# Different 64-byte starts for the weight-part buffers of a one-core hybrid decoder layer

## The chip, the core and the metric

The kernel runs on one core of one Trainium2 chip. The metric is the device time of one execution in microseconds; times of before are the median of three runs. The core has TensorE (matrix products), VectorE, ScalarE, GpSimd and SyncE, each with its own stream of instructions, and 16 DMA engines that they share. On-chip memory has 128 partitions; an address in this text is an offset in bytes within a partition, the same in all of them.

## The reference

One layer of a decoder trunk for 16 meta tokens and 256 tokens with 2048 channels, all in float32:

```python
u = rms_norm(h, g_pre_mix[l])
proj = u @ w_in[l]
z_pool, v_conv, g_conv, gate_a, gate_b = jnp.split(proj, splits, axis=-1)
y_a = causal_multiscale_pool(z_pool, w_pool_grp[l], pool_scale[l]) @ w_pool_out[l]
y_b = conformer_conv(v_conv, g_conv, w_dw[l], b_dw[l],
                     conv_ln_g[l], conv_ln_b[l]) @ w_conv_out[l]
m = jax.nn.sigmoid(gate_a) * y_a + jax.nn.sigmoid(gate_b) * y_b
h = h + rms_norm(m @ w_o[l], g_post_mix[l])
u = rms_norm(h, g_pre_mlp[l])
f = jnp.square(jax.nn.relu(u @ w_up[l])) @ w_down[l]
h = h + rms_norm(f, g_post_mlp[l])
```

w_in has 2048 x 7168 elements, w_up 2048 x 8192 and w_down 8192 x 2048. The result drops the meta tokens.

## The kernel before, in words

All weights are streamed once, in chunks of 1 MB (128 partitions x 2048 numbers, `CK` x `CW` or an equal area). A list `stream` holds them in order: w_in for the convolution's value and gate and for the pool (acc_v, acc_g, acc_z), w_in for the two gates (acc_gate), w_pool_grp, w_pool_out (acc_po), w_conv_out (acc_co), w_o (acc_o, acc_o_last), and then four rounds of w_up (acc_up) and w_down (acc_dn, at the end acc_f_last).

For accuracy each float32 operand is split in two parts of the faster type fp32r, a high part and the rest. `open_chunk` (line 136) takes the next chunk: SyncE loads it into a `raw` buffer (line 153), ScalarE writes the high part `hi` (line 156), VectorE writes `lo = raw - hi` (line 159). The activations (u, y, s_act, m, f_act) have two parts as well, at index a = 0 and 1. Three products are computed: high by high, high by low, low by high.

A matmul has a stationary operand (128 x 128 numbers, loaded by a weight load of its own) and a moving operand (128 x N, streamed through). Which part of a chunk is which depends on the stage:

- `block_t` (line 566; acc_gate, acc_po, acc_co, acc_o, acc_dn, acc_f_last): the activation is stationary, the weight chunk moves, mostly with N = 512. For each k the order is (a = 0, hi), (a = 0, lo), (a = 1, hi).
- `mm3` (line 308; acc_v, acc_g, acc_z): the weight chunk is stationary, u moves with N = 272. The order is (hi, a = 0), (hi, a = 1), (lo, a = 0).
- `mm2` (lines 313 and 318; acc_up): the weight chunk is stationary, u2 (the memory of m) moves; hi with both parts at once (N = 512), then lo with a = 0 (N = 256).

The order on each engine is that of the program, written out by hand; `fetch` (line 176) opens and splits chunks two ahead of the one that it hands out. VectorE's and ScalarE's other work stands between in queues (`pending`, `late`). Raws, hi and lo have three buffers each. Around the change from w_o to w_up, two chunks (numbers 90 and 91) get their parts in one buffer each of the tags s0 and s1 of the pool `big`, not in `parts`. Chunk 89 is the first of w_up and is in `parts`; 92 is the first after these two. Tags s0 and s1 later hold f_act, the MLP's activation: f_act0 (s0) has the first half of k of a round, f_act1 (s1) the second. Further lines named below: 652 and 641 (normalisation on VectorE), 796 and 800 (u2).

Pools follow one another in memory, in the order const, big, raws, parts, tmp; within a pool tags follow in the order of their first use. In the program before, u and m begin at 71,488, f_act1 (s1) at 106,304, f_act0 (s0) at 122,688, the raws at 139,072, and the parts at 163,648 and every 8,192 after it (three hi, then three lo). The tag of y and s_act begins at 21,376 and 37,760. A row of u for one k and a has 272 numbers, 1,088 = 17 x 64 bytes; acc_gate reads u from its 17th number on, 64 bytes into the row. The rows of m, y, s_act and f_act have 256 numbers for each k and a.

Of the kernel before, what the change touches and what calls it, by code (L numbers as in the profile page):

```python
# [9 lines left out]
F32R = mybir.dt.float32r  # L10
# [4 lines left out]
P = 128  # L15
CK = 4
CW = 512
# [5 lines left out]
def hybrid_block(ctx: ExitStack, tc: tile.TileContext, ins: dict, out: bass.AP):  # L23
# [3 lines left out]
    T, D = x.shape  # L27
# [3 lines left out]
    KD = D // P  # L31
    w_in = ins["w_in"][0]
    w_grp = ins["w_pool_grp"][0]
    NG, GD, _ = w_grp.shape
# [14 lines left out]
    const = ctx.enter_context(tc.tile_pool(name="const", bufs=1))  # L49
    big = ctx.enter_context(tc.tile_pool(name="big", bufs=1))  # L50
    raws = ctx.enter_context(tc.tile_pool(name="raws", bufs=3))
    parts = ctx.enter_context(tc.tile_pool(name="parts", bufs=3))
    tmp = ctx.enter_context(tc.tile_pool(name="tmp", bufs=2))
    psA = ctx.enter_context(tc.tile_pool(name="psA", bufs=6, space=PSUM))
    psB = ctx.enter_context(tc.tile_pool(name="psB", bufs=2, space=PSUM))
# [1 line left out]
    def f32(ap):  # L57
        return ap.bitcast(F32)
# [74 lines left out]
    opened = []  # L133
    at = {"n": 0}

    def open_chunk():
        n = at["n"]
        at["n"] += 1
        src, (rows, width) = stream[n]
        raw = raws.tile([P, CK * CW], F32, tag="raw", name=f"raw_{n}")  # L140
        if n in spare:
            both = big.tile([P, 2, CK * CW], F32R, tag=spare[n], name=f"parts_{n}")
            hi, lo = both[:, 0, :], both[:, 1, :]
        else:
            hi, lo = (parts.tile([P, CK * CW], F32R, tag=tag, name=f"{tag}_{n}")
                      for tag in ("hi", "lo"))
        raw, hi, lo = (t.rearrange("p (k c) -> p k c", k=rows) for t in (raw, hi, lo))
        pieces = rows if n < FIRST + 1 else 1
        k = rows // pieces
        loads = 4 if n < FIRST else 1  # L150
        for i in range(loads):
            sl = slice(i * rows // loads, (i + 1) * rows // loads)
            nc.sync.dma_start(raw[:, sl, :], src[:, sl, :])

        def high(sl):
            nc.scalar.copy(hi[:, sl, :], raw[:, sl, :])  # L156

        def low(sl):
            nc.vector.tensor_sub(lo[:, sl, :], raw[:, sl, :], f32(hi[:, sl, :]))  # L159

        def piece(i):
            def f():
                sl = slice(i * k, (i + 1) * k)
                high(sl)
                low(sl)
            return f
        todo = [piece(i) for i in range(pieces)]
        if n in spare:
            todo = [lambda: high(slice(0, rows)), lambda: low(slice(0, rows))]
        opened.append((hi, lo, todo))  # L170
# [5 lines left out]
    def fetch(ahead=2):  # L176

        for c in range(ahead + 1):
            if c == len(opened) and at["n"] < len(stream):
                open_chunk()  # L180
            if c < len(opened):
                split_pieces(c)
        flush()
        return opened.pop(0)[:2]
# [47 lines left out]
    for b in range(XB):  # L232
        load_x(b)
        if b % 2 == 0:
            open_chunk()
# [164 lines left out]
    def pieces_to(n):  # L400

        while first["split"] < min(n, (FIRST + 1) * HALF[0]):
            c = first["split"] // HALF[0]
            if c == at["n"]:
                open_chunk()
            opened[c][2].pop(0)()
            first["split"] += 1
# [212 lines left out]
    hi, lo = fetch()  # L620
# [185 lines left out]
    f_act = []  # L806
# [92 lines left out]
    for k0 in (3 * CK, 3 * CK + 2):  # L899
# [4 lines left out]
    up_high(2, 1)  # L904
    up_low(2)
    hi, lo = fetch()
    f_act += [big.tile([P, KD // 2, 2, T], F32R, tag=f"s{b}", name=f"f_act{b}")
              for b in range(2)]
    for j, acc in enumerate(accs):
        for k in range(CK):  # L910
            kk = 3 * CK + k
# [68 lines left out]
    n = KD // CK - 3  # L980
    for kc in range(n):
        hi, lo = fetch()
# [12 lines left out]
    for h, cs in enumerate(col_halves):  # L995
# [3 lines left out]
        s = tmp.tile([P, HALF_CW], F32, tag="sum", name=f"last_{h}")  # L999
# [37 lines left out]
```

## Time and profile before

| | us |
|---|---|
| median of three runs | 1256.38 |
| lowest, highest | 1256.12, 1256.86 |
| the profiled execution | 1256.48 |
| its span, first to last instruction | 1254.7 |

| engine | busy us | share of the span |
|---|---|---|
| TensorE matmuls (PE) | 1241.1 | 99% |
| TensorE weight loads (PEld) | 1064.9 | 85% |
| VectorE (DVE) | 810.2 | 65% |
| ScalarE (ACT) | 542.4 | 43% |

The DMA engines moved 237 MB at a mean of 189 GB/s. The granted TensorE clock is full throughout.

Matmuls are pipelined, so the duration that the profile gives one of them (around 390 ns for 512 columns) is not what it adds to the time. What it adds is the distance from one start to the next. That is read from the chain of work that ended last, whose rows give a start, a length and a count, or from rows of the timeline.

### The profile page before, as it was taken

How to read it: one execution, taken by the hardware profiler on the slowest of the kernel's cores; microseconds unless marked ns; L12 is line 12 of the kernel's file. 1: busy time of each engine (PE TensorE's matmuls, PEld its weight loads, DVE VectorE, ACT ScalarE, POOL GpSimd, SP SyncE). 2: the span in 40 equal slices, each digit the busy share in tenths (PEclk: the TensorE clock that was granted, in tenths of full speed). 3: DMA queues.
4: the chain of work that ended last, by engine and by line, in shares of the span. 5: the costliest groups of instructions: out<-in, count | busy, mean ns of one | idle time of the engine just before them, and what ended most of it. 6: DMA issues, size and time to landing. Idle time of an engine off the chain costs nothing.

```text
span 1254.7 us, 15708 instructions
## 1 busy us (share of the span) xinstructions
PE 1241.1 (99%) x6562; PEld 1064.9 (85%) x6562; DVE 810.2 (65%) x938; ACT 542.4 (43%) x571; POOL 6.1 (0%) x18
## 2 busy tenths in 40 slices
PE   8999999999999999999999999999999999999997
PEld 7999988888888888898888888888888888888886
DVE  5799978999676664585654456554465544556555
ACT  6633334443583434555533344433344433435432
POOL 1000000000000000000000000000000000000000
PEclk9999999999999999999999999999999999999999
DMA  7655555555547655646555655556656556556551
GB/s 244 207 184 180 168 176 194 194 178 200 171 165 285 214 205 201 201 140 197 189 181 200 201 175 194 183 188 200 198 171 202 180 190 200 181 189 198 179 192 68
DMA packets 130759, 237.24 MB, mean 189 GB/s; under 512 B 3985, under 2 KB 29905, under 8 KB 130160
## 3 DMA queue, kind: packets, MB, share of 16 engines
q1 hardware_dynamic: 129280, 230.70, 56.2%
q0 software_dynamic: 768, 4.35, 0.9%
q10 hardware_dynamic: 640, 1.19, 0.3%
q8 instruction: 51, 0.84, 0.3%
q14 instruction: 20, 0.16, 0.0%
HBM read 234.12 MB, written 2.10 MB: 188 GB/s over the span
## 4 chain that ended last, share of the span: by engine, by line
PE 98%; DVE 0%; DMA 0%; ACT 0%; DVEq 0%; ACTq 0%; issue 0%
PE acc_dn L566 26%; PE acc_up L313 19%; PE acc_gate L566 14%; PE acc_up L318 10%; PE acc_o L566 5%; PE acc_v L308 4%; PE acc_z L308 4%; PE acc_g L308 4%; PE acc_co L566 4%; PE acc_po L566 4%; PE acc_f_last L566 2%; PE acc_o_last L566 2%; PE xt L256 1%; DMA m_in<-in_meta_dram 0%; PE ht L790 0%; PE mt L685 0%
## 5 line engine op out<-in xcount | busy, mean ns | idle before, releaser
L159 DVE TENSOR_TENSOR lo<-raw,hi 128x2048 fp32r<-128x2048 f32 (+1 forms) x236 | 495.1, 2101 | 364.0 <-ACT hi L156 363.0
L156 ACT CAST hi<-raw 128x2048 fp32r<-128x2048 f32 (+1 forms) x236 | 413.9, 1757 | 574.0 <-PE acc_dn L566 191.1
L313 PE MATMUL acc_up<-m,hi 128*128 128x512 f32 (+1 forms) x1008 | 344.8, 395 | 0.0
L566 PE MATMUL acc_dn<-hi,f_act 128*128 128x512 f32 x960 | 296.4, 389 | 0.0
L318 PE MATMUL acc_up<-m,lo 128*128 128x256 f32 x992 | 265.8, 281 | 0.0
L313 PEld LDWEIGHTS acc_up<-m,hi 128*128 128x128 f32 x1008 | 183.2, 188 | 39.5
L566 PEld LDWEIGHTS acc_dn<-hi,f_act 128*128 128x128 f32 x960 | 180.2, 188 | 37.4
L318 PEld LDWEIGHTS acc_up<-m,lo 128*128 128x128 f32 x992 | 186.2, 189 | 6.3
L566 PE MATMUL acc_dn<-lo,f_act 128*128 128x512 f32 x480 | 186.7, 389 | 0.0
L566 PE MATMUL acc_gate<-hi,u 128*128 128x512 f32 x512 | 161.8, 396 | 0.0
L376 DVE SCALAR_TENSOR_TENSOR c<-a,taps,c 128x256 f32<-128x256 f32 x240 | 115.4, 483 | 6.6
L566 PEld LDWEIGHTS acc_gate<-hi,u 128*128 128x128 f32 x512 | 96.0, 188 | 22.4
L566 PEld LDWEIGHTS acc_dn<-lo,f_act 128*128 128x128 f32 x480 | 90.1, 188 | 18.6
L566 PE MATMUL acc_gate<-lo,u 128*128 128x512 f32 x256 | 99.9, 390 | 0.0
L566 PE MATMUL acc_o<-hi,m 128*128 128x512 f32 x192 | 59.5, 390 | 0.0
L566 PEld LDWEIGHTS acc_gate<-lo,u 128*128 128x128 f32 x256 | 48.1, 188 | 11.7
L308 PE MATMUL acc_v<-u,hi 128*128 128x272 f32 x256 | 51.1, 297 | 0.0
L308 PE MATMUL acc_g<-u,hi 128*128 128x272 f32 x256 | 48.3, 288 | 0.0
L308 PE MATMUL acc_z<-u,hi 128*128 128x272 f32 x256 | 48.3, 288 | 0.0
L566 PEld LDWEIGHTS acc_o<-hi,m 128*128 128x128 f32 x192 | 36.0, 188 | 7.4
L566 PE MATMUL acc_co<-hi,s_act 128*128 128x512 f32 x128 | 41.1, 397 | 0.0
L308 PEld LDWEIGHTS acc_v<-u,hi 128*128 128x128 f32 x256 | 40.9, 193 | 0.0
(222 smaller groups left out, 1062.8 us busy)
## 6 DMA issues: line engine op xcount, KB each, us to landing
raw<-in_w_up_dram SPq DMA_DIRECT2D x64, 1024.0 KB, 5.4
raw<-in_w_down_dram SPq DMA_DIRECT2D x64, 1024.0 KB, 5.1
raw<-in_w_in_dram SPq DMA_DIRECT2D x54, 1024.0 KB, 5.1
raw<-in_w_o_dram SPq DMA_DIRECT2D x16, 1024.0 KB, 5.1
raw<-in_w_pool_out_dram SPq DMA_DIRECT2D x8, 1024.0 KB, 5.2
raw<-in_w_conv_out_dram SPq DMA_DIRECT2D x8, 1024.0 KB, 5.2
x_in<-in_x_dram SPq DMA_DIRECT2D x4, 512.0 KB, 8.5
raw<-in_w_in_dram SPq DMA_DIRECT2D x8, 256.0 KB, 7.5
```

The source lines that it names most:

```text
L156: nc.scalar.copy(hi[:, sl, :], raw[:, sl, :])
L159: nc.vector.tensor_sub(lo[:, sl, :], raw[:, sl, :], f32(hi[:, sl, :]))
L256: nc.tensor.transpose(pt[:, M + t * P:M + (t + 1) * P], x_in[:, t, sl], ident)
L308: nc.tensor.matmul(acc, w[:, k[0], cs], act[:, k[1], a, off:], start=first and n == 0, stop=last and n == 2)
L313: nc.tensor.matmul(acc.rearrange("p (a t) -> p a t", a=2)[:, :, ts], hi[:, k[0], cs], act[:, k[1], :, off + ts.start:off + ts.stop], start ...
L318: nc.tensor.matmul(acc[:, :T], lo[:, k[0], cs], act[:, k[1], 0, off:], start=False, stop=False)
L376: nc.vector.scalar_tensor_tensor(c, conv["a"][:, q, i:i + T], taps[:, q, i:i + 1], c, op0=ALU.mult, op1=ALU.add)
L566: nc.tensor.matmul(acc, act(kk)[:, a_, ts_], w_[:, k, :], start=kk == 0 and n == 0, stop=kk == nk - 1 and n == 2)
```

## The change

The six buffers of `parts` get a tag each (hi0 to hi2, lo0 to lo2), with a room that is 0, 64, 128 or 192 bytes larger than the part, and the part lies at the end of its room. Which one a chunk gets is its number modulo 3. Before, each tag's three buffers were taken in turn by the chunks that use them, and chunks 90 and 91, which use none, weren't counted. f_act0 gets a room 64 bytes larger, too, and lies at its end, so the tag s0 grows by 64 bytes; f_act1 stays as it was. Everything behind a larger room in memory moves by as much.

```diff
-    parts = ctx.enter_context(tc.tile_pool(name="parts", bufs=3))
+    parts = ctx.enter_context(tc.tile_pool(name="parts", bufs=1))
...
+    SHIFT = {"hi0": 0, "hi1": 64, "hi2": 128, "lo0": 64, "lo1": 192, "lo2": 0}
+
+    def part_tile(tag, n):
+        key = f"{tag}{n % 3}"
+        room = parts.tile([P, CK * CW + SHIFT[key] // 4], F32R, tag=key, name=f"{tag}_{n}")
+        return room[:, SHIFT[key] // 4:]
+
     def open_chunk():
...
-            hi, lo = (parts.tile([P, CK * CW], F32R, tag=tag, name=f"{tag}_{n}")
-                      for tag in ("hi", "lo"))
+            hi, lo = (part_tile(tag, n) for tag in ("hi", "lo"))
...
-    f_act += [big.tile([P, KD // 2, 2, T], F32R, tag=f"s{b}", name=f"f_act{b}")
-              for b in range(2)]
+    for b in range(2):
+        room = big.tile([P, KD * T + 16 * (1 - b)], F32R, tag=f"s{b}", name=f"f_act{b}")
+        f_act.append(room[:, 16 * (1 - b):].rearrange("p (k a t) -> p k a t", k=KD // 2, a=2))
```

## The prediction

> **What bounds the kernel now.** I read the page first (share of each engine, then the chain that ended last), then the chain in order of time, then windows, waits and timelines of single stages.
>
> ```profile
> span 1254.7 us, 15708 instructions
> PE 1241.1 (99%) x6562; PEld 1064.9 (85%) x6562; DVE 810.2 (65%) x938; ACT 542.4 (43%) x571; POOL 6.1 (0%) x18
> PE 98%; DVE 0%; DMA 0%; ACT 0%; DVEq 0%; ACTq 0%; issue 0%
> ```
>
> The reader is to see that TensorE is never short of work: 98% of the chain is matmuls. So the time can move only if a matmul itself takes another time, or if a new wait opens in front of one. The profiled execution took 1256.48 us, 1.8 us more than its span and 0.1 us above the median of the three runs (1256.38); I make the sum against 1256.48.
>
> The chain in order of time gives the pace of each stage: length divided by count.
>
> ```profile
> 80.56 12.05 PE acc_g L308 x96
> 164.94 150.47 PE acc_gate L566 x648
> 350.67 44.80 PE acc_po L566 x192
> 425.22 11.20 PE acc_co L566 x48
> 449.22 59.86 PE acc_o L566 x264
> 625.38 87.05 PE acc_dn L566 x384
> 802.87 87.05 PE acc_dn L566 x384
> ```
>
> All but the first row are 512-column matmuls of one form, and their paces differ: acc_dn 226.7 ns, acc_o 226.7, acc_po and acc_co 233.3, acc_gate 232.2. The 272-column acc_g runs at 125.5. The two acc_dn pieces also give the up stage between them: 802.87 - (625.38 + 87.05) = 90.44 us for 256 pairs of a 512- and a 256-column matmul, 353.3 ns a pair.
>
> What makes 226.7 into 233.3? Not the clock and not the neighbours' work:
>
> ```profile
> 350.00:400.00 50.00, 50.00 (x219) 40.18 (x218) 34.12 (x28) 29.95 (x31) 1.27 (x2) 1.00 0.59 199
> 450.00:500.00 50.00, 50.00 (x222) 41.42 (x221) 23.95 (x15) 21.30 (x18) 0.30 (x1) 1.00 0.61 212
> 650.00:700.00 50.00, 50.00 (x222) 41.41 (x221) 24.26 (x14) 17.22 (x9) 0.00 (x0) 1.00 0.58 192
> ```
>
> The columns are the window, its length, then busy time and count of TensorE, weight load, VectorE, ScalarE and GpSimd, granted clock, DMA share, GB/s. The clock is 1.00 in all three, and DMA is 0.58 to 0.61. VectorE is busier in the first, which lies in acc_po, but acc_co at 425 us has the same 233.3 as acc_po at 350, whatever VectorE does beside them. What does separate the stages is where their operands begin. I count places in 64-byte units modulo 8. Before, every weight part (hi, lo), m and f_act begin at place 5, and y and s_act at place 6. While one matmul streams its moving rows, the weights of the next are being loaded (weight load is busy 85% of the span beside a busy TensorE). Let d be the place of those weights minus the place of the moving rows. acc_dn and acc_o have d = 0 throughout; acc_po and acc_co have d = 1. In the gates u has rows of 17 x 64 bytes, so d walks through all places: odd for two of the three matmuls of a k, even for the third.
>
> **Prices.** For 512 columns: d = 0 costs 226.7 ns; d odd 233.3 (6.67 more). Even but not zero follows from the gates: 3 x 232.2 - 2 x 233.3 = 230.0, 3.3 more. For this last the ends are 0 (it is like zero) and 6.67 (like odd); I take the 3.3 of the gates.
>
> On two reading streams the Trainium skill has a rule, in "TensorE: Matmul & The Clock Gate", Part 2, step 1: the array reads moving rows and weights through two independent ports, so loading the next weights takes nothing from the running matmul. By it d is worth nothing and the sum would be 0. The trace disagrees: 226.7 against 233.3 for one form. The same page's "Back-to-back issue gap" gives N/2.4 + 2.5 ns, 215.8 ns for 512 columns; no stage here comes under 226.7.
>
> **The change part by part.** No instruction, load or queue entry is added or removed. What moves are addresses, and one choice of buffer.
>
> *Where things come to lie.* With 64 bytes more in tag s0 the raws begin at place 6 and the parts pool at place 6; adding the room sizes in order of first use (hi0, lo0, hi1, lo1, hi2, lo2) gives hi0 6, lo0 7, hi1 0, lo1 3, hi2 5, lo2 5. f_act0 goes to 6, f_act1 stays at 5, u and m at 5, y and s_act at 6. The order of use is my assumption from the other tags of this kernel. Each stage meets all three buffers in turn, so I average over them.
>
> *acc_dn and acc_f_last (1440 + 144 matmuls).* Moving hi, lo, hi against f_act at 6 (first half of k) or 5. d for (hi, lo, hi): buffer 0: 0, 7, 0 and 7, 6, 7; buffer 1: 6, 3, 6 and 5, 2, 5; buffer 2: 1, 1, 1 and 0, 0, 0. Of 18: nine odd, four even, five zero. (9 x 6.67 + 4 x 3.3) / 18 = 4.07 ns each; x 1584 = +6.4 us. Ends: even free +5.3, even like odd +7.6.
>
> *acc_o (384).* m at 5: 7, 6, 7; 5, 2, 5; 0, 0, 0. Four odd, two even: 3.7 ns, +1.4 us (1.1 to 1.7).
>
> *acc_po, acc_co (384).* Weights at 6, all odd before; after: 0, 7, 0; 6, 3, 6; 1, 1, 1. Four of nine get cheaper, two by 6.67 and two by 3.3: -0.9 us (-1.1 to -0.6).
>
> *acc_gate (768).* With buffers 0 and 1 all three d are even: 230.0 in place of 232.2 for 512 matmuls, -1.1 us (-2.8 if even is free, at 226.7).
>
> *acc_v, acc_g, acc_z (1056 past the start).* Here u moves and hi, lo are loaded. One of three d was odd; with buffers 0 and 1 all three are: 1056 x 2/3 x 2/3 = 469 more odd ones. No row prices an odd d at 272 columns by itself: lower end 0, since the stage's 125.5 is one mean over odd and even; upper end 6.67 from acc_po, 3.1 us. The stage's own row is nearer in form but silent, so I take the middle, +1.6.
>
> *acc_up (976 pairs).* All d are 0 before, yet a pair takes 353.3. Zero-distance matmuls elsewhere say 226.7 + 120.0 = 346.7, the 120.0 from the last block:
>
> ```profile
> 1239.75 0.28 PE L566 MATMUL acc_f_last<-lo,f_act 128*128 128x256 f32 x1
> ...
> 1241.19 0.28 PE L566 MATMUL acc_f_last<-lo,f_act 128*128 128x256 f32 x1
> ```
>
> (five such rows 0.36 us apart, three matmuls each). So an up pair already pays 6.67 that I can't explain. With buffers 0 and 1 (651 pairs) the wide matmul gets d even (2 or 6) and the narrow one d odd (1 or 3). Upper end 3.3 + 6.67 = 10 ns a pair, +6.5 us; lower end, the unexplained 6.67 goes, -4.3 us. I take half the upper, +3.3: the narrow matmul is nearest to the 272-column stage, where I also took half.
>
> *The buffer choice.* Two chunks (90 and 91) lie in s0 and s1 and use no slot. Before, the slots simply went on; after, the chunk's number decides, so chunk 92 gets the buffer of chunk 89 and not that of 87. Its cast must wait for the last read of hi 89, its subtraction for the last of lo 89.
>
> ```profile
> 540.82 2.08 PE L318 MATMUL acc_up<-m,lo 128*128 128x256 f32 x16
> ```
>
> ```profile
> 544.39 1.93 ACT L156 CAST hi<-raw 128x2048 fp32r<-128x2048 f32 x1
> ```
>
> ```profile
> 547.29 2.28 DVE L159 TENSOR_TENSOR lo<-raw,hi 128x2048 fp32r<-128x2048 f32 x1
> ```
>
> The reads of hi 89 are over as the lo group starts (about 541.1), those of lo 89 at 542.9; the writers come at 544.39 and 547.29 anyway, 3.3 and 4.4 us later. Cost 0. Were that cover gone, chunk 92 would come later by what exceeds it, and with it what stands behind the cast and the subtraction on ScalarE and VectorE, the next u2 tiles and chunk 93.
>
> *VectorE, ScalarE and DMA.* Their operands come to lie apart, too.
>
> ```profile
> L159 DVE TENSOR_TENSOR lo<-raw,hi 128x2048 fp32r<-128x2048 f32 x212 | 485.6, 2291 | 363.6 <-ACT hi L156 362.7
> L159 DVE TENSOR_TENSOR lo<-raw,hi 128x256 fp32r<-128x256 f32 x24 | 9.4, 417 | 0.3 <-ACT hi L156 0.3
> L652 DVE TENSOR_TENSOR c<-c,sq 128x1024 f32<-128x1024 f32 x2 | 2.5, 1226 | 4.3 <-ACT c L647 4.3
> ```
>
> L159, with all operands at one place, takes (2291 - 417) / 1792 = 1.046 ns a column, so 1220 for 1024; L652, whose sq lies one place beyond c, takes 1226. A slower subtraction or cast would cost nothing, since the cast idles until TensorE frees its buffer:
>
> ```profile
> ACT hi L156 <- PE acc_dn L566: 191.1, 57, 3.5
> ACT hi L156 <- PE acc_up L313: 146.1, 45, 3.8
> ACT hi L156 <- PE acc_gate L566: 85.3, 25, 4.2
> ```
>
> *Sum.* 6.4 + 1.4 - 0.9 - 1.1 + 1.6 + 3.3 = +10.7 us: 1256.48 + 10.7 = 1267.2. All low ends: 5.3 + 1.1 - 1.1 - 2.8 + 0 - 4.3 = -1.8 (1254.7). All high ends: 7.6 + 1.7 - 0.6 - 1.1 + 3.1 + 6.5 = +17.2 (1273.7).
>
> **Rivals.**
>
> *Nothing happens.* The two streams don't meet, and 233.3 is due to something else in the pool- and conv-output stages. For it: the up pairs pay 6.67 at d = 0, so d isn't the whole story. Against it: acc_co at 425 us keeps 233.3 although the stage right behind it, acc_o, with the same form, runs at 226.7; and the gates with all d lie between. Time 1256.5. This is what the skill's two-port rule above would give.
>
> *Faster: the moving rows decide.* A 2048-byte row that begins at an even place may need one 64-byte step less than one at an odd place. Before, hi and lo begin at 5, odd, always. After, hi of buffers 0 and 1 begin even, for 4/9 of the matmuls that stream hi and lo: 704 of acc_dn and acc_f_last, 341 of acc_gate, 341 of acc_o, acc_po and acc_co. At 6.67 ns each that is -9.2 us: 1247.2. For it: every row above is of odd starts, so none contradicts it. Against it: acc_po differs from acc_o in its weights alone. It decides if it stands instead of the prices by d, or with them if it saves more than 10.7 / 1386 = 7.7 ns each.
>
> *Dearer: any d but zero costs as odd.* acc_dn, acc_f_last, acc_o at their upper ends, acc_up too: 1273.7, as summed.
>
> **How the numbers follow.** Sum by d 0.54, dearer 0.12, nothing 0.10, faster 0.24. Measurements of this kernel tell 0.2% (2.5 us) from no change. The sum's cases and the dearer one are slower, 0.66 together; the sum reaches "same" only with every end low, which I put with the nothing case: same 0.10. Predicted 1267.2, its own range 1259 to 1274. For 8 in 10 the range runs from 1250, with part of the faster rival, to 1274; about 0.13 lies below and 0.06 above.
>
> **What would show it.** The acc_dn piece of 384 goes from 87.05 to 88.6 us, acc_o's 264 from 59.86 to 60.8, acc_po's 192 from 44.80 to 44.4, acc_gate's 648 from 150.47 to 149.5, the up stage of 256 pairs from 90.44 to 91.3, acc_g's 96 from 12.05 to 12.2. Within acc_dn the pace should change from chunk to chunk with period three. If acc_dn gets shorter, the prices by d are wrong; if all paces stay, addresses don't matter; an idle stretch of TensorE between the up groups of the first project would mean that the buffer choice cost something. What I trust least is acc_up, whose pace I can't explain before.

## The result, and the profile after

The changed kernel takes 1258.88 us (median of 19 runs, 1258.15 to 1260.46) where the kernel before takes 1256.82 beside it: ratio 1.0016, 95% interval 1.0010 to 1.0023. It is slower, by 2.1 us. Forecast were +10.7 us, to 1267.2. The direction held, and the time lies in the wide range (1250 to 1274), just below the sum's own range (1259 to 1274). The size did not hold, and one term of the sum had the wrong sign.

The page of the changed kernel, first its span, then the busy times of the engines:

```profile
span 1257.0 us, 15708 instructions
PE 1243.1 (99%) x6562; PEld 1065.6 (85%) x6562; DVE 810.2 (64%) x938; ACT 541.6 (43%) x571; POOL 6.2 (0%) x18
```

The same instructions, and TensorE is as full as before: its busy time and the span grew by 2.0 and 2.3 us. So no wait was opened; the matmuls themselves take another time. The chain in order of time says where (start, length, what). The kernel after:

```profile
81.16 11.99 PE acc_g L315 x96
...
165.24 149.47 PE acc_gate L573 x648
...
349.75 44.55 PE acc_po L573 x192
...
447.84 60.73 PE acc_o L573 x264
508.57 20.74 PE acc_o_last L573 x90
...
624.48 88.72 PE acc_dn L573 x384
802.66 88.63 PE acc_dn L573 x384
980.70 88.75 PE acc_dn L573 x384
1158.96 66.53 PE acc_dn L573 x288
1225.50 22.46 PE acc_f_last L573 x144
```

and three rows of the same view of the kernel before that the prediction did not show:

```profile
509.08 20.40 PE acc_o_last L566 x90
...
1157.86 65.28 PE acc_dn L566 x288
1223.14 22.42 PE acc_f_last L566 x144
```

The reader is to go down the two lists and keep account of how late the second kernel is.

| stretch | measured | forecast |
|---|---|---|
| to the start of acc_gate (acc_v, acc_g, acc_z) | 165.24 - 164.94 = +0.30 | +1.6 |
| acc_gate, to the start of acc_po | 184.51 - 185.73 = -1.22 | -1.1 |
| acc_po, acc_co, to the 264 of acc_o | 98.09 - 98.55 = -0.46 | -0.9 |
| acc_o, acc_o_last | 0.87 + 0.34 = +1.21 | +1.4 |
| acc_up, first round | 95.17 - 95.90 = -0.73 | with the next |
| acc_up, three further rounds of 256 pairs | 89.46 + 89.41 + 89.51 - 3 x 90.44 = -2.95 | +3.3 |
| acc_dn, acc_f_last | 1.67 + 1.58 + 1.70 + 1.25 + 0.04 = +6.24 | +6.4 |
| sum | +2.4 | +10.7 |

The rounds of acc_up are the gaps between the pieces of acc_dn, as in the prediction (802.66 - 624.48 - 88.72 = 89.46). The first row holds a late start: acc_g's row at 81.16 is 0.60 late. The start of this row differs from run to run by more than that (80.34 in align and 82.69 in m_64 below, which leave the distances of this stage alone). From there to acc_gate the kernel after is 0.30 us the faster one.

Most of the miss is acc_up: -3.7 us where +3.3 was forecast. How it got faster shows in the timeline, in the rows of the first wide matmul of a chunk (16 pairs lie between one row and the next). The second round before:

```profile
712.26 0.39 PE L313 MATMUL acc_up<-m,hi 128*128 128x512 f32 x1
...
717.90 0.40 PE L313 MATMUL acc_up<-m,hi 128*128 128x512 f32 x1
...
723.55 0.40 PE L313 MATMUL acc_up<-m,hi 128*128 128x512 f32 x1
...
729.21 0.40 PE L313 MATMUL acc_up<-m,hi 128*128 128x512 f32 x1
```

and after:

```profile
713.04 0.39 PE L320 MATMUL acc_up<-m,hi 128*128 128x512 f32 x1
...
718.58 0.40 PE L320 MATMUL acc_up<-m,hi 128*128 128x512 f32 x1
...
724.14 0.39 PE L320 MATMUL acc_up<-m,hi 128*128 128x512 f32 x1
...
729.79 0.39 PE L320 MATMUL acc_up<-m,hi 128*128 128x512 f32 x1
```

Before, each chunk takes 5.64 to 5.66 us. After, the first (slot 1, the prediction's buffer 1) takes 5.54, the second (slot 2) 5.56 and the third (slot 0) 5.65. The second is the odd one: hi2 and lo2 lie at place 5, the place of the moving rows, exactly as before the change, and yet it is 0.08 to 0.10 us faster than the chunks before.

### The profile page after: what moved, and what is told of

It reads as the page before. It is cut to its first block, busy times and chain, and to the rows that moved or that the text cites. A ratio compares the mean times of both kernels' runs of the same rounds, so it can differ in the third digit from the quotient of the medians.

```text
span 1257.0 us, 15708 instructions
## 1 busy us (share of the span) xinstructions
PE 1243.1 (99%) x6562; PEld 1065.6 (85%) x6562; DVE 810.2 (64%) x938; ACT 541.6 (43%) x571; POOL 6.2 (0%) x18
## 4 chain that ended last, share of the span: by engine, by line
PE 98%; DMA 1%; DVE 0%; ACT 0%; DVEq 0%; ACTq 0%; issue 0%
PE acc_dn L573 26%; PE acc_up L320 19%; PE acc_gate L573 14%; PE acc_up L325 10%; PE acc_o L573 5%; PE acc_v L315 4%; PE acc_g L315 4%; PE acc_z L315 4%; PE acc_po L573 4%; PE acc_co L573 4%; PE acc_f_last L573 2%; PE acc_o_last L573 2%; PE xt L263 1%; DMA m_in<-in_meta_dram 1%; PE ht L797 0%; PE mt L692 0%
## 5 line engine op out<-in xcount | busy, mean ns | idle before, releaser
L166 DVE TENSOR_TENSOR lo<-raw,hi 128x2048 fp32r<-128x2048 f32 (+1 forms) x236 | 495.1, 2101 | 364.4 <-ACT hi L163 363.9
L163 ACT CAST hi<-raw 128x2048 fp32r<-128x2048 f32 (+1 forms) x236 | 413.1, 1754 | 576.0 <-PE acc_dn L573 197.5
L320 PE MATMUL acc_up<-m,hi 128*128 128x512 f32 (+1 forms) x1008 | 341.2, 389 | 0.0
L573 PE MATMUL acc_dn<-hi,f_act 128*128 128x512 f32 x960 | 300.2, 393 | 0.0
```

The source lines that it names most:

```text
L320: nc.tensor.matmul(acc.rearrange("p (a t) -> p a t", a=2)[:, :, ts], hi[:, k[0], cs], act[:, k[1], :, off + ts.start:off + ts.stop], start ...
L573: nc.tensor.matmul(acc, act(kk)[:, a_, ts_], w_[:, k, :], start=kk == 0 and n == 0, stop=kk == nk - 1 and n == 2)
```

## The experiments

The texts on record give some paces in cycles. They are read in proportion, with 544 for the 226.7 ns of a matmul of acc_dn: 816 are 340.0 ns, 832 are 346.7 and 848 are 353.3. Distances below are place of the weights minus place of the moving rows, modulo 8.

### The two parts of the change, each alone

f_only: f_act0 alone begins 64 bytes further; parts and all else stay where they were.

```diff
-    f_act += [big.tile([P, KD // 2, 2, T], F32R, tag=f"s{b}", name=f"f_act{b}")
-              for b in range(2)]
+    for b in range(2):
+        room = big.tile([P, KD * T + 128 * (1 - b)], F32R, tag=f"s{b}", name=f"f_act{b}")
+        f_act.append(room[:, 16 * (1 - b):16 * (1 - b) + KD * T].rearrange(
+            "p (k a t) -> p k a t", k=KD // 2, a=2))
```

> Only f_act0 moves, by 64 bytes; m, the parts and all else keep their places. Offset theory (a matmul's pace follows from d, the place of the weights being loaded minus that of the moving rows): in acc_dn the chunks on f_act0 have d = 1 and run at acc_po's 233.3 ns, those on f_act1 keep 226.7, so 384 matmuls take 88.3 us instead of 87.05; acc_up stays at 90.4 us for 256 pairs; the total rises by 720 x 6.67 ns = 4.8 us and 0.5 us in acc_f_last. Nothing-by-address theory: no change.

parts_only: the six tags and their rooms as in the change; f_act0 has its larger room but begins at the room's start.

```diff
-            hi, lo = (parts.tile([P, CK * CW], F32R, tag=tag, name=f"{tag}_{n}")
-                      for tag in ("hi", "lo"))
+            hi, lo = (part_tile(tag, n) for tag in ("hi", "lo"))
...
+        f_act.append(room[:, :KD * T].rearrange("p (k a t) -> p k a t", k=KD // 2, a=2))
```

> The changed kernel with f_act0 back at place 5; the parts stay where the change put them. If the parts alone make acc_up faster, its 256 pairs stay at 89.5 us; if f_act0 had a hand in it, they return towards 90.4. acc_dn should run as acc_o does in the changed kernel, 230.0 ns, 88.3 us for 384 instead of 88.7: the total falls by about 1.3 us against the changed kernel, to within 1.5 us of the kernel before.

f_only took 1262.40 us, ratio 1.0037 (1.0022 to 1.0051); parts_only 1257.25, ratio 1.0001 (0.9991 to 1.0010). The chain of f_only:

```profile
626.22 88.43 PE acc_dn L566 x384
805.10 88.43 PE acc_dn L566 x384
```

and of parts_only:

```profile
624.27 88.36 PE acc_dn L573 x384
802.09 88.27 PE acc_dn L573 x384
```

In f_only half of acc_dn's matmuls are at an odd distance and half at zero: 88.43 us is 230.3 ns each, the mean of 233.3 and 226.7 to 0.3 ns. The price of an odd distance in matmuls of one form is confirmed, and the 90.45 us of acc_up (805.10 - 626.22 - 88.43) show that f_act0 has no part in its gain. parts_only has all of it: 802.09 - 624.27 - 88.36 = 89.46. So the parts alone bring the whole gain in acc_up and most of the loss in acc_dn; f_act0's move on top of them adds 0.4 us a round to acc_dn (88.3 against 88.7).

### The price of an even distance, and an odd one undone

m_128 puts m 128 bytes further, so that acc_o is at distance 2 throughout; m_64 puts it 64 bytes further.

```diff
-    m = big.tile([P, KD, 2, T], F32R, tag="um", name="m")
+    m_room = big.tile([P, 2 * KD * T + 32], F32R, tag="um", name="m")
+    m = m_room[:, 32:].rearrange("p (k a t) -> p k a t", k=KD, a=2)
```

> Only m moves, by 128 bytes inside its buffer; no part and no f_act moves. acc_up then has d = 6 for both matmuls of every pair, acc_o d = 2 throughout. Offset theory: acc_o at the gates' even price, 230.0 ns, 264 in 60.7 us instead of 59.86; acc_up, where d = 0 gave 353.3, falls towards 347 with nothing else touched: 256 pairs in 88.8 us, the total falls by about 6.5 - 1.3 = 5 us. If the slow pace of acc_up comes from the reversed pair at a project's end and not from d, it stays at 90.4 us and the total rises by 1.3 us.

> Only m moves, by 64 bytes: d = 1 in acc_o, d = 7 for both matmuls of an up pair. Offset theory with the odd price: acc_o at 233.3 ns, 264 in 61.6 us; acc_up with an odd wide and an odd narrow matmul 353.3 or more, 256 pairs at 90.4 to 92.2 us. Rhythm theory: acc_up on one of its two steady paces, or between them as with m 128 bytes off (89.8).

The chain of m_128:

```profile
449.57 61.35 PE acc_o L566 x264
...
627.19 87.06 PE acc_dn L566 x384
804.04 87.06 PE acc_dn L566 x384
```

acc_o takes 232.4 ns at distance 2, nearly the odd price and not the 230.0 that the gates had suggested; at distance 1 (m_64) it takes 61.61 us, 233.4 ns. The total of m_128 is 1256.36 (ratio 0.9996, 0.9987 to 1.0005), since acc_up gives back what acc_o loses: 804.04 - 627.19 - 87.06 = 89.79 us with both hi and lo at distance 6 (88.8 was expected), and 90.15 in m_64 (one run, 1259.44) with both at 7. So leaving zero is dearer in acc_o and cheaper in acc_up, by the same edit.

align goes the other way: 64 bytes more in the tag "a" bring the parts to place 6, where y and s_act are, so acc_po and acc_co have distance 0. Everything behind "a" moves along and keeps its distances. align_no_rev is the same on no_rev (below).

```diff
-        conv["a"] = big.tile([P, KC, PAD + L], F32, tag="a", name="a")
+        a_room = big.tile([P, KC * (PAD + L) + 16], F32, tag="a", name="a")
+        conv["a"] = a_room[:, :KC * (PAD + L)].rearrange("p (q l) -> p q l", q=KC)
```

> Everything from the tag c on moves up by 64 bytes together, so that y and s_act, which stay, begin at the same place as the parts (6). Only acc_po's and acc_co's d changes, from 1 to 0. Offset theory: they fall from 233.3 to 226.7 ns, 192 from 44.80 to 43.5 us, the total by 384 x 6.67 ns = 2.6 us; acc_dn, acc_o, acc_gate and acc_up keep their paces. Nothing-by-address theory: no change.

> Both of the edits above at once: no offset between operands except in the gates and the first projections, and no two wide matmuls in a row in acc_up. By the offset theory -2.6 us; by the rhythm theory with a fast start -2.6 - 6.5 = -9.1 us, 1247.4.

The chain of align:

```profile
350.43 43.55 PE acc_po L567 x192
```

43.55 us are 226.8 ns each, against 233.3. align took 1254.52 us (ratio 0.9978, 0.9969 to 0.9988), align_no_rev 1254.62 (0.9978, 0.9969 to 0.9987), against 1257.22 for the kernel before beside them. The 384 matmuls of the two stages at 6.6 ns each make 2.5 us of the 2.7. The 1247.4 that align_no_rev would take if acc_up came into the fast pace by itself did not come.

### What makes acc_up faster

Two theories: either each chunk has the pace of its own distances, or it takes over the pace of the chunk ahead. third_only moves hi1 and lo1 alone, to the places that they have after the change (the 128 bytes of hi2 bring the buffers behind them back to place 5). part_tile and the six tags are those of the change, f_act0 is as before.

```diff
+    SHIFT = {"hi0": 0, "lo0": 0, "hi1": 192, "lo1": 192, "hi2": 128, "lo2": 0}
```

> Only hi1 and lo1 move, to the places that the change gives them (0 and 3); the other four parts and f_act0 stay at 5. Offset theory: in acc_up only every third chunk, the one in hi1 and lo1, falls from 353.3 to 347 ns a pair, the other two stay at 353.3; 256 pairs take 89.9 us. Rhythm theory (the pairs have two steady paces, 347 and 353 ns, and a chunk whose places allow both keeps the one that it is entered with): chunks in hi2, lo2 and hi0, lo0 that follow one in hi1, lo1 run at 347, too, until the last chunk of a project, whose last pair is in reverse order; 256 pairs take 89.4 to 89.5 us. Both: acc_dn pays 554.8 - 544 cycles in every third chunk, 228.2 ns on the mean, 87.6 us for 384, acc_gate gains 0.4 us, acc_o loses 0.6.

The chain of third_only:

```profile
625.51 87.58 PE acc_dn L573 x384
802.41 87.57 PE acc_dn L573 x384
```

1254.87 us, ratio 0.9983 (0.9973 to 0.9992): faster than both kernels. acc_up takes 802.41 - 625.51 - 87.58 = 89.32 us, as little as with the whole change. A third of the chunks, moved, brings all of the gain of acc_up, while acc_dn pays only 0.5 us a round instead of 1.7.

The last pair of each accumulation is turned round (low part first), so that two wide matmuls meet there. no_rev turns none.

```diff
-        if last:
-            mm2_low(acc, lo, act, k, cs)
-        mm2_high(acc, hi, act, k, cs, first, stop=last)
-        if not last:
-            mm2_low(acc, lo, act, k, cs)
+        mm2_high(acc, hi, act, k, cs, first)
+        mm2_low(acc, lo, act, k, cs, stop=last)
```

> No address moves. The last pair of each accumulation of acc_up runs in the order of the others, wide then narrow, so that no two wide matmuls (and no two narrow ones) follow one another. Offset theory: d stays 0, so acc_up stays at 353.3 ns a pair, 90.4 us for 256, and the total stays. Rhythm theory: the slow pace sets in behind two wide matmuls in a row, so without them a project keeps the pace that it begins with: if that is the fast one, 256 pairs take 88.8 us and the total falls by 6.5 us to 1250; if the stage before leaves it in the slow one, 90.4 stays.

It took 1257.17 us, ratio 0.9999 (0.9990 to 1.0008), and in its chain acc_up keeps 803.39 - 625.84 - 87.10 = 90.45 us:

```profile
625.84 87.10 PE acc_dn L563 x384
803.39 87.06 PE acc_dn L563 x384
```

So at distance 0 acc_up has the slow pace without the turned pairs, too. With them out of the way (all the kernels that follow stand on no_rev), kick moves hi1 and lo1 only while they carry acc_up, to distances 3 and 6; kick_hi moves hi1 alone, kick_lo lo1 alone; kick_align is kick with the edit of align.

```diff
+    def part_tile(tag, n):
+        up = n >= UP + 3 and (n - UP) // (NB * (KD // CK)) % 2 == 0
+        room = parts.tile([P, CK * CW + 128 * (n % 3 == 1)], F32R, tag=f"{tag}{n % 3}",
+                          name=f"{tag}_{n}")
+        skip = {"hi": 48, "lo": 96}[tag] if n % 3 == 1 and up else 0
+        return room[:, skip:skip + CK * CW]
```

UP is the number of the first chunk of w_up; parts has one buffer a tag, as in the change. In kick_hi the 96 is 0, in kick_lo the 48.

> No pair is turned round, as in no_rev, and only the buffers of slot 1 (every third chunk) lie elsewhere, and those only while they carry weights of acc_up: hi1 at place 0 and lo1 at place 3, against moving rows at place 5. Every other chunk, of acc_up in slots 0 and 2 and of acc_dn, acc_o, acc_gate in all slots, stands where it stood. Theory of two paces (a chunk keeps the pace in which it is entered; a slot-1 chunk at these places sets the fast one): after the first slot-1 chunk of a block every chunk runs at about 832 cycles a pair, the 256 pairs of acc_up between two blocks of acc_dn take 88.8 to 89.0 us instead of 90.45, acc_dn stays at 87.1, and the total falls by four times 1.5, to about 1250.5. Rival, that a place costs each matmul its own price: only the slot-1 chunks are faster, a third of 1.7 us, 89.9 between the blocks of acc_dn, total about 1254.5.

> kick and align together: y and s_act also begin at the place of the weight buffers. Theory: the two gains lie in different stages and add, 1250.5 less 2.6, about 1248, below both kernels; acc_po 43.55 us, 256 pairs of acc_up 88.8 to 89.0. Rival of single prices: about 1252.

> kick with hi1 alone at place 0 while it carries acc_up; lo1 stays at place 5, the place of the moving rows. If the place of the weights behind a narrow matmul (hi) sets the pace, acc_up takes 88.8 to 89.0 us as in kick; if the place of lo does, 90.45; if both are needed, between, and only in the slot-1 chunks.

> kick with lo1 alone at place 3 while it carries acc_up; hi1 stays at place 5. If the place of lo sets the pace, 88.8 to 89.0 us; if that of hi does, 90.45.

The timeline of kick, first wide matmul of the chunks in slots 1, 2, 0 and 1 again:

```profile
711.12 0.39 PE L321 MATMUL acc_up<-m,hi 128*128 128x512 f32 x1
...
716.67 0.40 PE L321 MATMUL acc_up<-m,hi 128*128 128x512 f32 x1
...
722.22 0.39 PE L321 MATMUL acc_up<-m,hi 128*128 128x512 f32 x1
...
727.77 0.39 PE L321 MATMUL acc_up<-m,hi 128*128 128x512 f32 x1
```

All three chunks take 5.55 us, the two that were not moved as well (5.65 and 5.66 before). The three gaps between the pieces of acc_dn are 88.82, 88.90 and 89.00 us: the third and fourth round begin with a chunk in slot 0 and in slot 2, and until the first chunk in slot 1 the chunks still take 5.64 and 5.65. kick took 1251.26 us, ratio 0.9955 (0.9942 to 0.9969), near the 1250.5 of the theory that a pace is kept and away from the 1254.5 of single prices. kick_align took 1249.49, ratio 0.9940 (0.9927 to 0.9954).

third_only has the same places in slot 1 (there in every stage), but turned pairs, and takes 89.32 to 89.56 us a round where kick takes 88.82 to 89.00. Its timeline shows the difference. Second wide matmuls of two chunks in a row, the first of them in slot 2 and right behind the turned pairs at the end of a project (four chunks):

```profile
735.50 0.40 PE L320 MATMUL acc_up<-m,hi 128*128 128x512 f32 x1
...
741.15 0.40 PE L320 MATMUL acc_up<-m,hi 128*128 128x512 f32 x1
```

These are 5.65 us; the same chunk of kick takes 5.55 (733.32 to 738.87). So the turned pairs, which the slow pace does not need, do end the fast one: behind them the chunks in slots 2 and 0 are slow until slot 1 comes again.

The same rows as those of kick, from kick_hi, beginning with the chunk in slot 2 of the second round (slots 2, 0, 1 and 2), and then the first chunk in slot 1 of the fourth round:

```profile
718.15 0.40 PE L321 MATMUL acc_up<-m,hi 128*128 128x512 f32 x1
...
723.80 0.40 PE L321 MATMUL acc_up<-m,hi 128*128 128x512 f32 x1
...
729.47 0.39 PE L321 MATMUL acc_up<-m,hi 128*128 128x512 f32 x1
...
734.91 0.40 PE L321 MATMUL acc_up<-m,hi 128*128 128x512 f32 x1
...
1076.73 0.40 PE L321 MATMUL acc_up<-m,hi 128*128 128x512 f32 x1
...
1082.33 0.40 PE L321 MATMUL acc_up<-m,hi 128*128 128x512 f32 x1
```

and of kick_lo, slots 2, 0, 1 and 2 of the second round:

```profile
717.69 0.40 PE L321 MATMUL acc_up<-m,hi 128*128 128x512 f32 x1
...
723.24 0.40 PE L321 MATMUL acc_up<-m,hi 128*128 128x512 f32 x1
...
728.79 0.39 PE L321 MATMUL acc_up<-m,hi 128*128 128x512 f32 x1
...
734.39 0.40 PE L321 MATMUL acc_up<-m,hi 128*128 128x512 f32 x1
```

These two fit neither theory whole. With hi1 alone moved, its own chunks take 5.44 us, 340 ns a pair, which no run had shown before; the unmoved chunks behind them fall back to 5.65 and 5.67. There is one exception, the last two rows: that moved chunk takes 5.60, 350 ns a pair. With lo1 alone moved, its own chunks take 5.60, and the unmoved ones behind them 5.55: they do better than the chunk that changed them. So distances 0 and 0 allow two paces, 5.65 and 5.55 us a chunk, and what ran ahead decides which; distances 3 and 0 mostly have a pace better than both. kick_hi took 1253.81 us and kick_lo 1252.44, one run each.

### hi moved in every slot

340 ns is 1.5 times the 226.7 of a 512-column matmul at distance 0: what 768 columns take at that pace. hi_all gives every chunk of acc_up that is in parts the places of kick_hi's moved ones; hi_all_1 and hi_all_2 do so with 64 and 128 bytes instead of 192 (STEP 16 and 32), and hi_all_align has the edit of align as well. The lo buffers stand still, and in every other stage all stand at the common place.

```diff
+    STEP = 48
+    ROOM = {"hi0": STEP, "hi1": 128 - STEP, "hi2": STEP}
+
+    def part_tile(tag, n):
+        up = n >= UP and (n - UP) // (NB * (KD // CK)) % 2 == 0
+        key = f"{tag}{n % 3}"
+        t = parts.tile([P, CK * CW + ROOM.get(key, 0)], F32R, tag=key, name=f"{tag}_{n}")
+        skip = {"hi0": STEP * up, "hi1": (128 - STEP) * (not up), "hi2": STEP * up}.get(key, 0)
+        return t[:, skip:skip + CK * CW]
...
-            hi, lo = (parts.tile([P, CK * CW], F32R, tag=tag, name=f"{tag}_{n}")
-                      for tag in ("hi", "lo"))
+            lo = part_tile("lo", n) if n % 3 != 1 else None
+            hi = part_tile("hi", n)
+            lo = lo if n % 3 != 1 else part_tile("lo", n)
```

The last lines set the order in memory (lo0, hi0, hi1, lo1, lo2, hi2), so that the larger rooms leave every lo at the common place.

> kick_hi in all three slots: while they carry acc_up, hi0, hi1 and hi2 lie 192 bytes (three places) behind the place of the moving rows, lo0, lo1 and lo2 at their place; in every other stage all stand where they stood. No pair is turned round. If the place of hi alone gives the pace of the chunk (816 cycles a pair in kick_hi, 1.5 times the 544 of a matmul of acc_dn, in each moved chunk), all chunks run at 816: 256 pairs in 87.04 us instead of 90.45, and with some 976 pairs the total falls by 13.0 us, to about 1244. If that pace came from the change of places between chunks, moved beside unmoved, it is lost and acc_up takes between 88.8 and 90.5: 1250 to 1257.

> hi_all with align: the gains add, 1244 less 2.6, about 1241.4, acc_po 43.55 us and 256 pairs of acc_up 87.04. Otherwise 1247 to 1254.

> hi_all with 64 bytes instead of 192. If any odd distance of hi does it, 816 cycles a pair and 87.04 us as in hi_all; if it is this one distance (three places), 88 to 91 us.

> hi_all with 128 bytes. If an odd distance of hi is what counts, about 848 cycles a pair, 90.45 us; if every distance but zero does it, 87.04 us.

The chain of hi_all:

```profile
623.21 87.06 PE acc_dn L575 x384
797.33 87.06 PE acc_dn L575 x384
```

and of hi_all_2:

```profile
624.65 87.07 PE acc_dn L575 x384
801.83 87.09 PE acc_dn L575 x384
```

hi_all: 797.33 - 623.21 - 87.06 = 87.06 us for 256 pairs, 340.1 ns each, in 1244.47 us, ratio 0.9887 (0.9838 to 0.9936; the interval is wide because one of the 11 runs of before beside it took 1272.22). hi_all_align took 1241.70, ratio 0.9866 (0.9832 to 0.9900), the fastest of all, 15.4 us under the kernel before beside it. hi_all_2 has 801.83 - 624.65 - 87.07 = 90.11 us, nearly the old pace, in 1254.86 us (one run). hi_all_1 took 1245.58 (one run), and its timeline has two paces: first two rows of the first round, 28 pairs apart, then two of the second, 16 apart.

```profile
551.59 0.40 PE L325 MATMUL acc_up<-m,hi 128*128 128x512 f32 x1
...
561.39 0.39 PE L325 MATMUL acc_up<-m,hi 128*128 128x512 f32 x1
...
722.39 0.39 PE L325 MATMUL acc_up<-m,hi 128*128 128x512 f32 x1
...
727.83 0.39 PE L325 MATMUL acc_up<-m,hi 128*128 128x512 f32 x1
```

9.80 us for 28 pairs are 350 ns, 5.44 for 16 are 340: the same buffers, places and instructions, at two paces. With lo at distance 0, the odd distances 1 and 3 of hi reach 340 and the even ones 0 and 2 do not. At both odd ones 350 was seen, too: for the whole first round of hi_all_1, and in one chunk of kick_hi. With lo moved as well an odd hi was not as good: 90.15 us for 256 pairs with both at 7 (m_64).

## Why the prediction was right or wrong

**That operands' places set the matmul's time** was right, and so was the way there: stages of one form, in one program, at two paces. f_only and m_64 each moved one buffer by 64 bytes, align all that lies behind one, and acc_dn, acc_o and acc_po moved by what was forecast. The rival in which nothing happens is out. The rule of the Trainium skill weighed there ("TensorE: Matmul & The Clock Gate", Part 2, step 1: two independent read ports, so that loading the next weights takes nothing from the running matmul) does not hold for these matmuls: f_only moves f_act0 alone, the weights of half of acc_dn's matmuls, and a piece of 384 takes 88.43 us in place of 87.05.

**acc_dn and acc_f_last** (+6.4 forecast, +6.2 measured), **acc_o** (+1.4, +1.2) and **acc_gate** (-1.1, -1.2) came out. The period of three is there: acc_gate's chunks take 230.0, 230.0 and 232.1 ns a matmul in turn, acc_o's 232.5, 231.3 and 226.7. In the first term the parts missed a little and made up for each other: acc_dn got 6.20 where its 1440 matmuls had 5.9 in the sum, acc_f_last 0.04 where it had 0.6. 96 of the 144 matmuls of acc_f_last are 256 wide; the prediction priced all of them as 512 wide.

**The price of an even distance** was read wrongly. A row of u moves by one place, so of the gates' even distances a quarter are zero, and 230.0 is a mean that includes them. Without them the same rows give (4 x 230.0 - 226.7) / 3 = 231.1 ns, and by itself an even distance costs acc_o 232.4 (m_128). **acc_po and acc_co** gained half of what was forecast (-0.46 for -0.9). third_only, with slot 1 moved alone, has acc_po at 44.56 us against 44.55 with the whole change, so the two matmuls of three that slot 0 brings to distance 0 gained nothing there. For mixed orders of distances a price for each matmul is only a rough rule.

**acc_v, acc_g, acc_z** was mis-sized: +1.6 forecast, and the stage lost nothing; from acc_g's row to acc_gate it gained 0.30 us, at worst +0.30 from the start of the kernel. More odd distances do not slow the 272-column matmuls here. The lower end taken in the prediction, 0, was the right one.

**acc_up is the step that failed**: "the narrow matmul is nearest to the 272-column stage, where I also took half", +3.3. It measured -3.7. The prediction carried a price for odd distances from stages of equal matmuls into one that alternates wide and narrow. There an odd distance of hi, loaded beside the narrow matmul, is the better one while lo stays at 0 (340 ns a pair against 353.3), and the slow pace at distance 0, which the prediction noted as 6.67 ns that it couldn't explain, was not a floor but one of two paces open to the same places. The lower end given, -4.3, was what would follow if these 6.67 went away; that is near what happened. kick and third_only show how: slot 1 sets the faster pace and slot 2 keeps it; after the change slot 0, whose places differ again, ends it (5.65 us), and so do the turned pairs.

**The buffer choice** cost nothing, as forecast: between acc_o_last and acc_dn the kernel after is faster, and TensorE's share of the span is unchanged. The subtraction takes 2101 ns in the mean in both pages and the cast 1754 after 1757, so operands at different places cost VectorE and ScalarE nothing there. **The rival that moving rows starting at even places are faster** is out: acc_dn got slower with them. **The dearer rival** had the price of an even distance nearly right (232.4 of 233.3 in m_128), but not acc_up's sign.

With -3.7 in place of +3.3, and the first stage at +0.3, the prediction's own sum would be 6.4 + 1.4 - 0.9 - 1.1 + 0.3 - 3.7 = +2.4, what the spans show. That the measured time lies in the wide range is partly luck: its lower end, 1250, was drawn for the rival of even starts, which is out.

## What to carry to other kernels

Where a stage of back-to-back matmuls runs slower per matmul than another of the same form with no wait between, compare the start addresses of the weights being loaded and of the rows being streamed: here 64 bytes are worth 3% of acc_po or acc_o and 64 or 192 bytes 4% of a round of acc_up, and the better offset differs from stage to stage (equal places where all matmuls are 512 wide; where 512 alternates with 256, hi 64 or 192 bytes off and lo at the place of the moving rows). Take such a price only from a stage with the same order of shapes. A buffer that stages share can lie at another offset in each, as in hi_all_align, which takes 1.2% less than the kernel before (1241.70 against 1257.14 us).

## What the runs showed that was not expected

One order of instructions on one set of addresses can run at two steady paces and keep the one that it comes in with: 350 and 340 ns a pair in hi_all_1, 353 and 347 at distance 0 (before, and behind the moved chunks of kick and kick_lo). In m_64, too, each of the last three rounds begins at 5.58 to 5.59 us a chunk and, behind its first turned pairs, goes on at 5.65 to 5.66, while the whole first round runs at 5.58 with turned pairs in it. A matmul's price is therefore not a function of its own addresses alone. What in the chip holds the pace, and why hi behind the narrow matmul is the better at an odd distance, no run here shows; that is left open.
